# A layer kernel's first loads: the last three weight tiles of the shift as column sums, other buffers and order of the loads, and the token tiles' scale put into their transposing product

## The chip, the cores and the metric

One core of one Trainium2 chip runs the kernel. The metric is the device time of one execution in microseconds, the median of several executions.

## What is computed

One layer of a generator. 1024 latent tokens `x` and 256 context tokens `ctx`, each 1024 wide, are normalised, scaled and shifted (scale and shift come from `silu(c) @ w_ada`) and go through one input projection `w_in`; then come window attention, a chunked mLSTM, an output projection and a SwiGLU block. The change touches the beginning:

```python
mod_x = (silu_c @ w_ada[layer] + b_ada[layer])[:, None, :]      # 1024 -> 6 x 1024
mod_c = silu_cc @ w_ada[layer] + b_ada[layer]
sh_m, sc_m, gt_m, sh_f, sc_f, gt_f = jnp.split(mod_x, 6, axis=-1)
px = modulate(rms_norm(x, g_pre_mix[layer]), sh_m, sc_m) @ w_in[layer]     # h * (1 + sc) + sh
pc = modulate(rms_norm(ctx, g_pre_mix[layer]), csh_m, csc_m) @ w_in[layer]
```

Everything is float32. The large products are made from two float32r halves of each operand (`split`: the high half by a copy on ScalarE, the low one by a subtraction on VectorE) in three matmuls (`mm3`: high by high, high by low, low by high).

## The kernel before, in words

All DMAs are issued by one queue (SP), in the order that the program's scheduler gives them; `tc.issue_after(d)` keeps a load behind another one in that queue. The scheduler also orders the instructions of each engine. The stages at the start are these.

**Scale and shift (the loop `for sec in (1, 0)`).** Section 1 of `w_ada` gives the scale, section 0 the shift. Each section is eight tiles `wa` of 128x1024 (512 KB). An even tile is, in float32, the moving operand of two matmuls of 512 columns against `cz4`, four columns of silu values; an odd tile is split first and takes four float32r matmuls against `cs4`. All add into `pr`, two banks of four rows. At a section's end `pr` is copied to a tile of four rows `r4` (half by ScalarE, half by VectorE), turned into columns by eight small transposes (`pcol`), and a few VectorE instructions make `scol` (scale) or `hcol` (shift) of them.

**Token tiles (`prep_a`, `prep_b`).** There are ten tiles of 128 tokens, eight of `x` and two of `ctx`. `prep_a(i)` loads `xt`, squares and sums it on ScalarE, takes the root there and the reciprocal on VectorE, and multiplies the whole tile by it on GpSimd (line 187). `prep_b(i)` turns the tile over in eight TensorE transposes (`pt<-cst,xt`, line 200), multiplies by `scol` on VectorE (line 202), adds `hcol` on GpSimd (line 203; on VectorE for tile 0), and splits the result into `hh` and `hl` (`ch` and `cl` for the context), the stationary operands of the projection.

**First projection (`s1`, lines 70 to 72).** Per token tile 24 matmuls of 272 columns against `w1h` and `w1l`, whose weights come in four loads of 272 KB (`slab_load`) behind all of `w_ada`. The loop runs `prep_a(i + 4)`, `prep_b(i + 2)` and `s1(i)`. Token tiles and first projection together are called stage 1 below.

**Behind it** come the second projection (`w2h`, `w2l`, 384 columns), the gates' chain and the rest of the layer. In a name such as `pt<-cst,xt` of a matmul the moving operand stands first and the stationary one second.

Of the kernel before, what the change touches and what calls it, by code (L numbers as in the profile page):

```python
# [9 lines left out]
F32 = mybir.dt.float32  # L10
F32R = mybir.dt.float32r
# [26 lines left out]
def body(tc, x, ctx, vecs, bcv, bada, gqm, gqf, wada, ws1, ws2, wt, wout, wfi, wfo,  # L38
# [68 lines left out]
    act.activation(csil, vec[:, VSIL:VSIL + 16].rearrange("p (k t) -> p k t", t=2), AF.Silu)  # L107
    convw = vec[:, VCONV:VCONV + 12].rearrange("p (i t) -> p i t", t=3)
# [30 lines left out]
    pool.memset(Vc[:, :, :, 128:129], 1.0)  # L139
# [8 lines left out]
    ch = [R(i, f"ch{i}", (4, L), F32R) for i in range(2)]  # L148
    cl = [R(2 + i, f"cl{i}", (4, L), F32R) for i in range(2)]
# [11 lines left out]

# [10 lines left out]
    xts, hraw, xd = {}, {}, {}  # L172
# [6 lines left out]
    def prep_a(i):  # L179

        j = i - NT
        xt = xts[i] = R(4 + i % 4, f"xt{i}", (D,))
        xd[i] = dma(xt, x[i * P:(i + 1) * P] if i < NT else ctx[j * P:(j + 1) * P])
        hraw[i] = R((12, 13, 8, 9, 10, 11)[i % 6], f"hraw{i}", (KT, P))
        act.activation(hraw[i].rearrange("p a b -> p (a b)"), xt, AF.Square, accum_out=st[:, i:i + 1])
        rms_r(st[:, 10 + i:11 + i], st[:, i:i + 1])
        pool.tensor_scalar(xt, xt, st[:, 10 + i:11 + i], 1.0, MUL, MUL)

    def prep_b(i):

        xt = xts.pop(i)
        q, j = (0, i) if i < NT else (1, i - NT)
        hs, ls = (hh, hl) if i < NT else (ch, cl)
        tok = slice(j * P, (j + 1) * P)
        rw = hraw.pop(i)
        for b in range(2):
            pt = pa.tile([P, 4, P], F32, name="pt", tag="tp", bufs=2)
            for k in range(4):
                kk = 4 * b + k
                pe.transpose(pt[:, k, :], xt[:, kk * P:(kk + 1) * P], ident)  # L200
            raw = rw[:, 4 * b:4 * b + 4]
            dve.tensor_tensor(raw, pt, hcast(scol[:, q, 4 * b:4 * b + 4]), MUL)
            (dve if i == 0 else pool).tensor_tensor(raw, raw, hcast(hcol[:, q, 4 * b:4 * b + 4]), ADD)
            split(hs[b][:, :, tok], ls[b][:, :, tok], raw)
# [5 lines left out]

    for sec in (1, 0):
        pr = [pa.tile([4, 512], F32, name=f"pr{sec}{i}", tag="mm", bufs=4) for i in range(2)]
        for kt in range(KT):
            w = R((8, 9, 10, 11, 12, 13)[(kt + 2 * (1 - sec)) % 6], f"wa{sec}_{kt}", (D,))
            wd = dma(w, wada[kt * P:(kt + 1) * P, sec * D:(sec + 1) * D])
            if kt % 2:
                wh, wl = (w2_tile(p, kt // 2 % 2, f"wa{p}{sec}_{kt}")[:, 0:D] for p in "hl")
                split(wh, wl, w)
                ops = ((cs4, wh), (cs4, wl))
            else:  # L220
                ops = ((cz4, w),)
            for n, (a, b) in enumerate(ops):
                for i in range(2):
                    pe.matmul(pr[i], a[:, kt, :], b[:, i * 512:(i + 1) * 512], start=kt == 0,
                              stop=kt == KT - 1 and n == len(ops) - 1)
            if (sec, kt) == (1, 0):
                with tc.issue_after(wd.ins):
                    dma(cst, const)
                    dma(bcr, bcast(bcv))
                dve.tensor_scalar(mF, up, -1.0, -NEG, ADD, MUL)  # L230
                dve.tensor_scalar(mB, lw, -1.0, -NEG, ADD, MUL)
            if (sec, kt) == (0, 4):
                prep_a(0)
        r4 = R((7, 6)[sec], f"r4_{sec}", (D,))[0:4]
# [15 lines left out]
    with tc.issue_after(wd.ins):  # L250
        for i in range(2):
            slab_load(w1h[i], w1l[i], ws1[:, i], 272, 2 * i)
# [33 lines left out]
    with tc.issue_after(wd.ins):  # L286
        for n in range(1, 4):
            prep_a(n)
    for n in range(2):
        prep_b(n)  # L290
# [1486 lines left out]
```

## Time and profile before

| what | value |
| --- | --- |
| median of 3 executions (lowest to highest) | 1234.12 us (1230.72 to 1235.18) |
| the profiled execution: its time, its span | 1231.71 us, 1229.9 us |
| TensorE busy | 1193.5 us, 97% of the span |
| VectorE, ScalarE, GpSimd busy | 799.9, 578.1, 205.8 us |
| mean granted TensorE clock | 0.996 of full speed |

The profile is of one execution. PE is TensorE's matmuls, PEld its weight loads, DVE VectorE, ACT ScalarE, POOL GpSimd, SP the queue that issues the DMAs. A matmul's duration in a row holds its way through the array, so consecutive ones overlap: what one costs in a stream is the distance between starts. A float32 matmul of the program is two instructions in the rows (the 32 of line 224 on `wa,cz` are 16 of the program), a float32r matmul or a transpose is one.

### The profile page before, as it was taken

To read this page: it belongs to the slowest core of one execution; us is meant where nothing else is said; L and a number is where in the kernel's file an instruction comes from. 1 tells how busy PE (TensorE), PEld (TensorE's weight loads), DVE (VectorE), ACT (ScalarE), POOL (GpSimd) and SP (SyncE) were. 2 spreads that over 40 slices of the span, in tenths; PEclk is the share of its full clock that TensorE was granted. 3 is DMA by queue.
4 is the path that set the end of the run, shared out by engine and by line. 5 is a ranking of instruction groups with operands and counts; after the bars stand their busy time and mean duration, and the time that the engine had idled before them with its cause. 6 is when DMAs were issued, how large, how long until landed. Compare 5 with 4: busy or idle time off the path is not lost.

```text
span 1229.9 us, 16238 instructions
## 1 busy us (share of the span) xinstructions
PE 1193.5 (97%) x5859; PEld 968.9 (79%) x5859; DVE 799.9 (65%) x1385; ACT 578.1 (47%) x1105; POOL 205.8 (17%) x245
## 2 busy tenths in 40 slices
PE   7889999999999998999999999999999999999997
PEld 1779878877777776887778888888888888888886
DVE  3882177772877788446867677767777755554567
ACT  3754533211766786587643333334333334444443
POOL 0651410235544476000000000000000000000000
PEclk9899999999999999999999999999999999999999
DMA  8542854556533320522034465575645548665853
GB/s 313 168 132 70 280 188 144 181 145 191 153 90 87 112 78 10 188 86 86 18 104 136 180 218 198 204 246 195 230 141 177 176 162 279 205 205 188 299 188 129
DMA packets 91096, 202.30 MB, mean 164 GB/s; under 512 B 9092, under 2 KB 29956, under 8 KB 89608
## 3 DMA queue, kind: packets, MB, share of 16 engines
q1 hardware_dynamic: 91016, 201.27, 49.4%
q8 instruction: 46, 0.75, 0.2%
q14 instruction: 34, 0.28, 0.1%
HBM read 149.85 MB, written 50.73 MB: 163 GB/s over the span
## 4 chain that ended last, share of the span: by engine, by line
PE 78%; DMA 7%; DVE 7%; POOL 3%; ACT 3%; issue 2%; SPq 1%; DVEq 0%; POOLq 0%; ACTq 0%
PE xv L72 8%; PE xv L70 8%; PE xv L71 8%; PE pt L70 5%; PE pt L71 5%; PE pt L72 5%; PE pt L708 2%; PE pt L707 2%; PE pt L808 2%; DMA wb<-in_wada 2%; PE op L72 2%; PE fx L70 2%; PE fx L71 2%; PE fx L72 2%; PE op L71 2%
## 5 line engine op out<-in xcount | busy, mean ns | idle before, releaser
L59 DVE TENSOR_TENSOR fo<-fr,fo 128x1024 fp32r<-128x1024 f32 x77 | 92.7, 1222 | 70.9 <-ACT fo L58 67.7
L58 ACT CAST fo<-fr 128x1024 fp32r<-128x1024 f32 x77 | 79.5, 1050 | 74.0 <-PE pt L72 34.9
L441 PE MATMUL t<-hh,th 128*128 128x512 f32 x208 | 82.5, 397 | 1.8 <-ACT cr L458 1.8
L442 PE MATMUL t<-hl,th 128*128 128x512 f32 x208 | 82.1, 395 | 0.0
L1192 ACT CAST wS<-wr 128x512 fp32r<-128x512 f32 x88 | 54.1, 622 | 55.8 <-PE pt L72 37.5
L1194 DVE TENSOR_TENSOR wS<-wr,wS 128x512 fp32r<-128x512 f32 x88 | 60.3, 688 | 20.7 <-ACT wS L1192 20.7
L444 PE MATMUL t<-hh,tl 128*128 128x512 f32 x208 | 68.2, 393 | 0.0
L70 PE MATMUL xv<-tT,wS 128*128 128x512 f32 x168 | 66.0, 393 | 0.0
L72 PE MATMUL xv<-tT,wS 128*128 128x512 f32 x168 | 65.6, 391 | 0.0
L71 PE MATMUL xv<-tT,wS 128*128 128x512 f32 x168 | 65.5, 390 | 0.0
L492 DVE SCALAR_TENSOR_TENSOR acc<-wb,csil,acc 128x1024 f32<-128x1024 f32 x24 | 33.9, 1411 | 40.6 <-DMA wb<-in_wada 40.6
L441 PEld LDWEIGHTS t<-hh,th 128*128 128x128 f32 x208 | 39.1, 188 | 10.4 <-ACT cr L458 2.4
L944 DVE TENSOR_TENSOR wr<-wr 128x512 f32<-128x512 f32 x66 | 45.5, 689 | 1.4
L442 PEld LDWEIGHTS t<-hl,th 128*128 128x128 f32 x208 | 39.1, 188 | 8.1 <-issue 1.2
L1226 ACT ACTIVATE es<-es 128x512 f32<-128x512 f32 x22 | 13.9, 633 | 66.6 <-DVE es L947 66.6
L72 PE MATMUL op<-woh,ml 128*128 128x512 f32 x112 | 43.8, 391 | 0.8 <-DVE ml L59 0.8
L444 PEld LDWEIGHTS t<-hh,tl 128*128 128x128 f32 x208 | 38.3, 188 | 7.9 <-issue 1.0
L70 PE MATMUL op<-woh,mh 128*128 128x512 f32 x112 | 44.2, 395 | 0.0
L71 PE MATMUL op<-wol,mh 128*128 128x512 f32 x112 | 43.7, 390 | 0.0
L70 PE MATMUL pt<-fo 128*128 128x512 f32 x110 | 42.8, 389 | 0.0
L71 PE MATMUL pt<-fo 128*128 128x512 f32 x110 | 42.8, 389 | 0.0
L72 PE MATMUL pt<-fo 128*128 128x512 f32 x110 | 42.8, 389 | 0.0
(991 smaller groups left out, 3489.9 us busy)
## 6 DMA issues: line engine op xcount, KB each, us to landing
wr<-in_wfi SPq DMA_DIRECT2D x44, 512.0 KB, 4.8
wb<-in_wada SPq DMA_DIRECT2D x24, 512.0 KB, 4.3
s_d<-a SPq DMA_DIRECT2D x22, 512.0 KB, 6.6
bt<-in_wfo SPq DMA_DIRECT2D x44, 256.0 KB, 3.7
tb_d<-bt SPq DMA_DIRECT2D x11, 1024.0 KB, 4.1
fr<-s_d SPq DMA_DIRECT2D x44, 256.0 KB, 4.5
fr<-tb_d SPq DMA_DIRECT2D x44, 256.0 KB, 4.3
fr<-a_d SPq DMA_DIRECT2D x33, 256.0 KB, 4.2
```

The source lines that it names most:

```text
L58: act.copy(hi, raw)
L59: dve.tensor_tensor(lo, raw, hi.bitcast(F32), SUB)
L70: pe.matmul(ps, a[0], b[0], start=first, stop=False, **kw)
L71: pe.matmul(ps, a[0], b[1], start=False, stop=False, **kw)
L72: pe.matmul(ps, a[1], b[0], start=False, stop=last, **kw)
L441: pe.matmul(o, wh[:, kt], m[0], start=f, stop=False)
L442: pe.matmul(o, wh[:, kt], m[1], start=False, stop=False)
L444: pe.matmul(o, wl[:, kt], m[0], start=False, stop=l)
L492: dve.scalar_tensor_tensor(a, t, csil[:, kt, 0:1], a, MUL, ADD)
L944: dve.tensor_tensor(out, a, b, SUB)
L1192: act.copy(w[:, 0], raw)
L1194: dve.tensor_tensor(w[:, 1], raw, w[:, 0].bitcast(F32), SUB)
```

## The change

- Of section 0 (the shift) five tiles go through `pr`, tiles 1, 3 and 4 of them split. Tiles 5, 6 and 7 become stationary operands: for each of the eight 128-column blocks of a tile there is one float32 matmul against two columns of silu values (`pcc<-csil,wa`, line 293 after). The sums stand in columns at once, and VectorE adds them to `hcol` (line 296 after).
- `w_ada` has a buffer for each of a section's eight tiles instead of six. `xt0` is loaded behind tile 1 of section 0, `xt1` behind tile 4; then come the first half of `w1`'s weights, tiles 5 to 7, and the second half, each half as one load of 544 KB into a buffer of its own.
- `prep_a` no longer multiplies the token tile: GpSimd multiplies the 128x128 unit matrix by the reciprocal root (`dg`, line 189 after), and `prep_b` has, for each transpose, a float32 matmul of the tile with `dg` (`pt<-dg,xt`, line 203 after).
- A Sqrt activation is added at the start, some instructions are kept in program order, `r4` lies in the memory of `Vc`, and the low halves of the second half of `w1` are made between the splits of tile 0.

```diff
@@ -105,6 +105,7 @@
     up, lw = cst[:, CUP:CUP + P], cst[:, CLO:CLO + P]
     sel, ind = cst[:, CSEL:CSEL + P], cst[:, CIND:CIND + 64]
     act.activation(csil, vec[:, VSIL:VSIL + 16].rearrange("p (k t) -> p k t", t=2), AF.Silu)
+    act.activation(st[:, 63:64], epst, AF.Sqrt)
...
@@ -145,8 +145,7 @@
-    ch = [R(i, f"ch{i}", (4, L), F32R) for i in range(2)]
-    cl = [R(2 + i, f"cl{i}", (4, L), F32R) for i in range(2)]
+    ch, cl = [], []
...
@@ -158,7 +157,7 @@
+    q1.tile([P, P], F32, name="dgx", tag="dg", bufs=4)
...
@@ -181,57 +180,89 @@
         j = i - NT
         xt = xts[i] = R(4 + i % 4, f"xt{i}", (D,))
         xd[i] = dma(xt, x[i * P:(i + 1) * P] if i < NT else ctx[j * P:(j + 1) * P])
-        hraw[i] = R((12, 13, 8, 9, 10, 11)[i % 6], f"hraw{i}", (KT, P))
-        act.activation(hraw[i].rearrange("p a b -> p (a b)"), xt, AF.Square, accum_out=st[:, i:i + 1])
+        hraw[i] = R((2, 3)[i] if i < 2 else (12, 13, 8, 9, 10, 11)[i % 6], f"hraw{i}", (KT, P))
+        sq = act.activation(hraw[i].rearrange("p a b -> p (a b)"), xt, AF.Square, accum_out=st[:, i:i + 1])
+        if i > 1:
+            tc.keep_in_program_order(sq)
         rms_r(st[:, 10 + i:11 + i], st[:, i:i + 1])
-        pool.tensor_scalar(xt, xt, st[:, 10 + i:11 + i], 1.0, MUL, MUL)
-
-    def prep_b(i):
-
-        xt = xts.pop(i)
+        dg[i] = q1.tile([P, P], F32, name=f"dg{i}", tag="dg", bufs=4)
+        pool.tensor_scalar(dg[i], ident, st[:, 10 + i:11 + i], 1.0, MUL, MUL)
+
+    def prep_b(i, between=None):
+
+        xt, dg_ = xts.pop(i), dg.pop(i)
         q, j = (0, i) if i < NT else (1, i - NT)
         hs, ls = (hh, hl) if i < NT else (ch, cl)
         tok = slice(j * P, (j + 1) * P)
         rw = hraw.pop(i)
+        tail = []
         for b in range(2):
             pt = pa.tile([P, 4, P], F32, name="pt", tag="tp", bufs=2)
             for k in range(4):
                 kk = 4 * b + k
-                pe.transpose(pt[:, k, :], xt[:, kk * P:(kk + 1) * P], ident)
+                pe.matmul(pt[:, k, :], xt[:, kk * P:(kk + 1) * P], dg_, start=True, stop=True)
             raw = rw[:, 4 * b:4 * b + 4]
             dve.tensor_tensor(raw, pt, hcast(scol[:, q, 4 * b:4 * b + 4]), MUL)
             (dve if i == 0 else pool).tensor_tensor(raw, raw, hcast(hcol[:, q, 4 * b:4 * b + 4]), ADD)
-            split(hs[b][:, :, tok], ls[b][:, :, tok], raw)
+            tail.append((hs[b][:, :, tok], ls[b][:, :, tok], raw))
+            if i:
+                h_, l_, raw = tail.pop()
+                tc.keep_in_program_order(act.copy(h_, raw))
+                dve.tensor_tensor(l_, raw, h_.bitcast(F32), SUB)
+        for b, t in enumerate(tail):
+            split(*t)
+            between(2 * b)
...
 
+
+    w1r = {}
+
+    def w1_load(i):
+        w1r[i] = R(i, f"wr1_{i}", (4, 272))
+        return dma(w1r[i], ws1[:, i])
+
+    def w1_hi(i, k):
+        act.copy(w1h[i][:, k:k + 2], w1r[i][:, k:k + 2])
+
+    def w1_lo(i, k):
+        return dve.tensor_tensor(w1l[i][:, k:k + 2], w1r[i][:, k:k + 2], w1h[i][:, k:k + 2].bitcast(F32), SUB)
+
+    PLAIN = {1: (0, 2, 4, 6), 0: (0, 2)}
+    NROW = {1: KT, 0: KT - 3}
+    last, nsp = None, 0
     for sec in (1, 0):
         pr = [pa.tile([4, 512], F32, name=f"pr{sec}{i}", tag="mm", bufs=4) for i in range(2)]
-        for kt in range(KT):
-            w = R((8, 9, 10, 11, 12, 13)[(kt + 2 * (1 - sec)) % 6], f"wa{sec}_{kt}", (D,))
-            wd = dma(w, wada[kt * P:(kt + 1) * P, sec * D:(sec + 1) * D])
-            if kt % 2:
-                wh, wl = (w2_tile(p, kt // 2 % 2, f"wa{p}{sec}_{kt}")[:, 0:D] for p in "hl")
+        for kt in range(NROW[sec]):
+            w = R(8 + kt, f"wa{sec}_{kt}", (D,))
+            with tc.issue_after(last) if last is not None else ExitStack():
+                last = dma(w, wada[kt * P:(kt + 1) * P, sec * D:(sec + 1) * D]).ins
+            if kt in PLAIN[sec]:
+                ops = ((cz4, w),)
+            else:
+                wh, wl = (w2_tile(p, nsp % 2, f"wa{p}{sec}_{kt}")[:, 0:D] for p in "hl")
+                nsp += 1
                 split(wh, wl, w)
                 ops = ((cs4, wh), (cs4, wl))
-            else:
-                ops = ((cz4, w),)
             for n, (a, b) in enumerate(ops):
                 for i in range(2):
                     pe.matmul(pr[i], a[:, kt, :], b[:, i * 512:(i + 1) * 512], start=kt == 0,
-                              stop=kt == KT - 1 and n == len(ops) - 1)
+                              stop=kt == NROW[sec] - 1 and n == len(ops) - 1)
             if (sec, kt) == (1, 0):
-                with tc.issue_after(wd.ins):
+                with tc.issue_after(last):
                     dma(cst, const)
-                    dma(bcr, bcast(bcv))
+                    last = dma(bcr, bcast(bcv)).ins
                 dve.tensor_scalar(mF, up, -1.0, -NEG, ADD, MUL)
                 dve.tensor_scalar(mB, lw, -1.0, -NEG, ADD, MUL)
-            if (sec, kt) == (0, 4):
-                prep_a(0)
-        r4 = R((7, 6)[sec], f"r4_{sec}", (D,))[0:4]
+            if (sec, kt) in ((0, 1), (0, 4)):
+                i = kt // 4
+                with tc.issue_after(last):
+                    prep_a(i)
+                    last = xd[i].ins
+        r4 = Vc.rearrange("p n h v -> p (n h v)")[0:4, 0:D]
         act.copy(r4[:, 0:512], pr[0])
         dve.tensor_copy(r4[:, 512:D], pr[1])
         pc_ = pa.tile([P, KT, 4], F32, name="pcol", tag="gx", bufs=2)
@@ -247,9 +278,29 @@
                 dve.tensor_tensor(t, t, vec[:, VGPM:VGPM + 8], MUL)
             else:
                 dve.tensor_tensor(t, t, bcol(0), ADD)
-    with tc.issue_after(wd.ins):
-        for i in range(2):
-            slab_load(w1h[i], w1l[i], ws1[:, i], 272, 2 * i)
+        if sec == 0:
+            with tc.issue_after(last):
+                last = w1_load(0).ins
+            for k in (0, 2):
+                w1_hi(0, k)
+                w1_lo(0, k)
+            pcc = pa.tile([P, KT, 2], F32, name="pcc", tag="mm", bufs=4)
+            for kt in range(NROW[0], KT):
+                w = R(8 + kt, f"wa{sec}_{kt}", (D,))
+                with tc.issue_after(last):
+                    last = dma(w, wada[kt * P:(kt + 1) * P, 0:D]).ins
+                for j in range(KT):
+                    pe.matmul(pcc[:, j, :], w[:, j * P:(j + 1) * P], csil[:, kt, :], start=kt == NROW[0] and j == 0,
+                              stop=kt == KT - 1, skip_group_check=j > 0)
+    for q in range(2):
+        dve.tensor_tensor(hcol[:, q], pcc[:, :, q], hcol[:, q], ADD)
+    pool.memset(Vc[:, :, :, 128:129], 1.0)
+    with tc.issue_after(last):
+        last = w1_load(1).ins
+    for k in (0, 2):
+        w1_hi(1, k)
+    ch += [R(i, f"ch{i}", (4, L), F32R) for i in range(2)]
+    cl += [R(2 + i, f"cl{i}", (4, L), F32R) for i in range(2)]
@@ -283,11 +334,13 @@
 
     NI = NT + NC_
     w2h, w2l = [], []
-    with tc.issue_after(wd.ins):
-        for n in range(1, 4):
+    prep_b(0, lambda k: tc.keep_in_program_order(w1_lo(1, k)))
+    for n in (2, 3):
+        with tc.issue_after(last):
             prep_a(n)
-    for n in range(2):
-        prep_b(n)
+        last = xd[n].ins
+        if n == 2:
+            prep_b(1)
     for i in range(NI):
         if i + 4 < NI:
             prep_a(i + 4)
```

Where the instructions stand. On TensorE, from the transposes of tile 0 to the first projection, before (`xt_248`, `xt_313` and `xt_320` are the token tiles 0, 1 and 2):

```order
L200 MATMUL pt<-cst,xt_248 128x128 x6
L224 MATMUL pr_214<-wal_7_272,cs_126 4x512
L224 MATMUL pr_215<-wal_7_272,cs_126 4x512
L239 MATMUL pcol<-cst,r_0_279 128x4 x8
L200 MATMUL pt<-cst,xt_313 128x128 x8
L70 MATMUL slab<-w1h_121,hh_101 128x272
L71 MATMUL slab<-w1l_123,hh_101 128x272
L200 MATMUL pt<-cst,xt_320 128x128 x8
L72 MATMUL slab<-w1h_121,hl_103 128x272
```

and in the changed kernel (`xt_258` is token tile 1; `pr_210` and `pr_211` are section 0):

```order
L252 MATMUL pr_210<-wah_4_250,cs_123 4x512
L252 MATMUL pr_211<-wah_4_250,cs_123 4x512
L252 MATMUL pr_210<-wal_4_251,cs_123 4x512
L252 MATMUL pr_211<-wal_4_251,cs_123 4x512
L270 MATMUL pcol<-cst,Vc 128x4 x4
L203 MATMUL pt<-dg_264,xt_258 128x128 x8
L270 MATMUL pcol<-cst,Vc 128x4 x4
L293 MATMUL pcc<-csil,wa_5_290 128x2 x8
L293 MATMUL pcc<-csil,wa_6_300 128x2 x8
L293 MATMUL pcc<-csil,wa_7_310 128x2 x8
L70 MATMUL slab<-w1h_117,hh_101 128x272
```

The products of tile 1 and the column sums of three tiles now stand ahead of the first projection, in this order, and the turning of token tile 2 no longer stands right behind its first two matmuls.

On VectorE, at the end of the shift, in the changed kernel (`hraw_228` is token tile 0, `w1l_120` the second half of `w1`):

```order
L280 TENSOR_TENSOR hcol<-hcol,vec 128x8 x2
L296 TENSOR_TENSOR hcol<-pcc,hcol 128x8 x2
L206 TENSOR_TENSOR hraw_228<-hraw_228,hcol 128x512 x2
L59 TENSOR_TENSOR hl_103<-hraw_228,hh_101 128x4x128
L232 TENSOR_TENSOR w1l_120<-wr_1_323,w1h_118 128x2x272
L59 TENSOR_TENSOR hl_104<-hraw_228,hh_102 128x4x128
L232 TENSOR_TENSOR w1l_120<-wr_1_323,w1h_118 128x2x272
```

The addition of the column sums is the last step ahead of token tile 0, whose splits and the rest of `w1l` stand behind it.


## Rows read from the trace of the kernel before

**Rows 1.** Busy time of each engine in three stretches of the span (start:end, length, then busy us and count of PE, PEld, DVE, ACT and POOL, the granted clock as a share of full speed, the DMA engines' share and GB/s).

```profile
40.00:50.00 10.00, 8.63 (x54) 8.01 (x54) 9.93 (x16) 8.25 (x18) 9.21 (x7) 0.74 0.44 152
42.20:84.20 42.00, 36.91 (x273) 35.01 (x274) 37.71 (x72) 25.71 (x56) 35.28 (x29) 0.96 0.42 129
84.20:163.00 78.80, 78.35 (x444) 71.88 (x443) 24.98 (x59) 37.27 (x96) 22.84 (x22) 1.00 0.54 180
```

**Rows 2.** Groups of instructions in the stretch from 42.2 to 84.2 us (line, engine, operation, tiles, shapes, count | busy us, mean ns | idle before them and what ended it).

```profile
L203 POOL TENSOR_TENSOR hraw<-hraw,hcol 128x512 f32<-128x512 f32 x18 | 25.2, 1410 | 6.6 <-DVE hraw L202 6.6
L72 PE MATMUL slab<-w1h,hl 128*128 128x272 f32 x64 | 19.5, 307 | 3.3 <-DVE hl L59 3.3
L187 POOL TENSOR_SCALAR xt<-xt,st 128x1024 f32<-128x1024 f32 x8 | 11.9, 1484 | 1.8 <-PE pt L200 1.8
L202 DVE TENSOR_TENSOR hraw<-pt,scol 128x512 f32<-128x512 f32 x17 | 11.4, 675 | 0.0
L200 PE MATMUL pt<-cst,xt 128*128 128x128 f32 x64 | 10.3, 293 | 0.2 <-POOL xt L187 0.2
L70 PE MATMUL slab<-w1h,ch 128*128 128x272 f32 x6 | 1.8, 307 | 1.5 <-ACT ch L58 1.5
```

**Rows 3.** PE in order of time, at the shift's matmuls and at the start of the first projection (start us, busy us, engine, line, operation, tiles, shapes, count, idle before).

```profile
24.25 0.75 PE L239 MATMUL pcol<-cst,r 4*128 4x4 f32 x8
...
26.28 1.88 PE L224 MATMUL pr<-wa,cz 128*4 128x512 f32 x4
28.09 0.63 PE L224 MATMUL pr<-wah,cs 128*4 128x512 f32 x2
...
29.11 1.88 PE L224 MATMUL pr<-wa,cz 128*4 128x512 f32 x4
...
42.23 0.60 PE L70 MATMUL slab<-w1h,hh 128*128 128x272 f32 x1 [1.19 <-ACT hh L58]
...
42.85 1.91 PE L200 MATMUL pt<-cst,xt 128*128 128x128 f32 x8
44.41 0.58 PE L72 MATMUL slab<-w1h,hl 128*128 128x272 f32 x1
...
45.21 0.28 PE L72 MATMUL slab<-w1h,hl 128*128 128x272 f32 x1
45.34 0.29 PE L70 MATMUL slab<-w1h,hh 128*128 128x272 f32 x1
45.46 0.29 PE L71 MATMUL slab<-w1l,hh 128*128 128x272 f32 x1
```

**Rows 4.** PE in order of time, a group of eight transposes in the middle of stage 1, and what follows it.

```profile
49.69 1.09 PE L200 MATMUL pt<-cst,xt 128*128 128x128 f32 x8 [0.18 <-POOL xt L187]
50.54 0.37 PE L72 MATMUL slab<-w1h,hl 128*128 128x272 f32 x1
```

**Rows 5.** PE in order of time in the mLSTM stage: float32 matmuls of 129 columns, each of the program's as two instructions.

```profile
343.31 0.49 PE L708 MATMUL pt<-V,wl 128*128 128x129 f32 x2
343.73 0.49 PE L707 MATMUL pt<-cs,qp 64*128 64x129 f32 x2
344.14 0.49 PE L708 MATMUL pt<-V,wl 128*128 128x129 f32 x2
```

**Rows 6.** PE in order of time: eight float32 matmuls of one column with 128x128 stationary operands, and what follows them.

```profile
193.45 1.84 PE L508 MATMUL ar<-one,acc 128*128 128x1 f32 x16
195.16 0.48 PE L442 MATMUL t<-hl,th 128*128 128x512 f32 x1
```

**Rows 7.** ACT in order of time: two copies that waited for their `w_ada` tile (tile 1 of section 1, tile 1 of section 0), the copy of a section's sums, a square with its read-out, the root with the table load ahead of it, the copy that waited for the last `w_ada` tile, and two copies of a half token tile.

```profile
9.01 1.04 ACT L58 CAST wah<-wa 128x1024 fp32r<-128x1024 f32 x1 [6.08 <-DMA wa<-in_wada]
...
20.68 1.05 ACT L58 CAST wah<-wa 128x1024 fp32r<-128x1024 f32 x1 [1.62 <-DMA wa<-in_wada]
23.62 0.58 ACT L235 COPY r<-pr 4x512 f32<-4x512 f32 x1 [1.89 <-PE pr L224]
...
28.20 1.06 ACT L185 ACTIVATE hraw<-xt 128x1024 f32<-128x1024 f32 x1 [2.92 <-PE pr L224]
29.16 0.19 ACT L185 ACTIVATION_READ_ACCUMULATOR hraw<-xt 128x1 f32 x1
...
30.30 1.28 ACT L176 ACT_TABLE_LOAD   x1
31.59 0.29 ACT L176 ACTIVATE st<-st,epst 128x1 f32<-128x1 f32 x1
32.38 1.04 ACT L58 CAST wah<-wa 128x1024 fp32r<-128x1024 f32 x1 [0.49 <-DMA wa<-in_wada]
...
41.58 1.12 ACT L58 CAST hh<-hraw 128x512 fp32r<-128x512 f32 x2
```

**Rows 8.** DVE in order of time: a reciprocal, the shift's last step, and the addition of the shift to half a token tile.

```profile
31.92 0.17 DVE L177 RECIPROCAL st<-st 128x1 f32<-128x1 f32 x1 [0.38 <-ACT st L176]
39.07 0.25 DVE L249 TENSOR_TENSOR hcol<-hcol,vec 128x8 f32<-128x8 f32 x2
39.88 0.68 DVE L203 TENSOR_TENSOR hraw<-hraw,hcol 128x512 f32<-128x512 f32 x1
```

**Rows 9.** POOL in order of time: the nearest smaller and larger size of a product by a column.

```profile
7.53 0.20 POOL L637 TENSOR_SCALAR bcr<-bcr 128x8 f32<-128x8 f32 x1 [6.12 <-DMA bcr<-in_bcv]
37.90 1.12 POOL L187 TENSOR_SCALAR xt<-xt,st 128x1024 f32<-128x1024 f32 x1 [4.61 <-DVE st L177]
```

More of the change, by code (lines that the diff above doesn't have):

```diff
@@ L138, in body @@
     pool.memset(V[:, :, :, 128:129], 1.0)
-    pool.memset(Vc[:, :, :, 128:129], 1.0)
     pool.memset(G, 0.0)
@@ L170, in w2_tile @@
         return q1.tile([P, 4 * 384], F32R, name=name, tag=f"w2{part}{i}")
-    xts, hraw, xd = {}, {}, {}
+    xts, hraw, xd, dg = {}, {}, {}, {}
     def rms_r(dst, ss):
```

## The prediction, made before the change was run

> **What bounds the kernel now.** I read the busy time by stretches first: it tells in which part of the span TensorE has room [rows 1]. From 84.2 to 163 us PE is busy 78.35 of 78.80 us, and the whole page has it at 97%. So a microsecond that the start wins or loses is passed on to the end nearly whole. From 42.2 to 84.2 us three engines are close together: PE 36.91, DVE 37.71 and POOL 35.28 of 42.00 us. The groups of that stretch say what PE lacks there [rows 2]: its matmuls waited 3.3 us for `hl`, 1.5 us for the context's `ch` and 0.2 us for `xt`, 5.0 us together. Behind those waits stands GpSimd, with 1484 ns for each scaled tile and two additions of 1410 ns, 4.3 us a token tile. Third, PE in order of time gives the start of the first projection [rows 3]: its first matmul is at 42.23. Two things are to be seen behind it. The transposes of token tile 2 (the third one) take from 42.85 to 44.41, 1.56 us, and the five slab matmuls around them are slow: 42.23 to 42.85 (two) and 44.41 to 45.21 (three) are 1.42 us, where the later ones start 0.125 us apart (45.21 to 45.46), 0.62 for five. That is 0.8 us lost; the stretch from 40 to 50 has a granted clock of 0.74 [rows 1], a mixture of the levels 1.2 and 2.4 GHz.
>
> **The price of turning a tile.** Before, eight transposes take 0.85 us in the stream (49.69 to 50.54), 0.106 each [rows 4]. After, each is an ordinary float32 matmul with a 128x128 stationary operand and 128 moving columns. The nearest row is the mLSTM's: 128x128 against 129 columns, two instructions, from one pair to the next 0.42, 0.41 us [rows 5]. I take 0.417 us: 3.34 us a tile instead of 0.85. Lower bound: the columns alone, without any weight load. 512 float32 columns are 0.45 us an instruction (26.28 to 28.09 for four) [rows 3], 128 columns twice are 0.226 us. Upper bound: the pair's own 0.49 us [rows 5]. I take the middle because shape, type and stream are the same there.
>
> A rule bears on this. In the row, the columns explain 0.226 of 0.417 us, and the rest is what a weight load costs when it stands alone: eight matmuls of one column take 1.71 us (193.45 to 195.16), 0.107 us an instruction [rows 6]. So in float32 the loads of successive blocks were not hidden. The Trainium skill, TensorE: Matmul & The Clock Gate, Part 2: What happens when you issue a matmul, says that the engine pulls a weight load ahead of matmuls that are under way, so that the next weights load meanwhile. By that rule a product would cost its columns alone, and the sum below would end near 1235 us instead of 1248. The pairs' 0.417 us speak against it here.
>
> **The change, part by part.**
>
> Until PE has done the first copies of tile 1 of the shift, the order on PE is the same, so I keep 24.25 us for the start of `pcol` [rows 3] and walk from there in the new order. Half of `pcol` 0.4 (half of 0.75), the low half of tile 1 0.5 (half of 28.09 to 29.11), tile 2 of the shift 1.8, the other half of `pcol` 0.4: 27.35. `dg` of token tile 0 must be there: the copy of the sums ends at 24.2, square and read-out 1.25, table load 1.28, root 0.29 [rows 7], reciprocal 0.17 [rows 8], and the product of the unit matrix between 0.20 (8 columns) and 1.12 us (1024 columns) [rows 9]; with 128 columns I take 0.3. That is 27.5, and the Sqrt at the program's start does not remove the table load, since the Silu behind it loads another table. Products of tile 0 3.34: 30.85. Shift tiles 3 and 4, both split, 2.0: 32.85. Copy of the sums 0.6: 33.45, half of `pcol` 33.85. Products of tile 1 3.34: 37.2, `pcol` 37.6. Then the column sums: 24 float32 matmuls, 48 instructions of 0.107 us [rows 6], 5.1: 42.7. The row has one column, here are two; were they as dear as 129 columns it would be 10.0, were they free 0. Then 0.25 for the two additions to `hcol`, 0.68 for the shift of half a tile [rows 8], 0.6 for its copy (41.58, two in 1.12) [rows 7] and 0.25 for hand-overs: the first projection starts at 44.5 instead of 42.23, **+2.3**.
>
> The loads do not set this. Between 9.01 and 20.68 nine loads of 512 KB landed, 1.30 us each [rows 7]. In the new order tile 7 of the shift comes 16 such loads and one of 544 KB (1.4) behind tile 1 of section 1: 31.2, against 32.38 before [rows 7], though `xt1` and half of `w1` now stand ahead of it in SP's queue. PE comes to it after 40 us; a slip of 8 us in the queue costs nothing. The second half of `w1` lands at 32.6 and token tile 2 at 33.9, also early. Two SP issues fewer for `w1`, and two splits of 128x1024 fewer with one more for tile 4, are worth nothing for the same reason: ScalarE and VectorE have waits in that stretch. If PE were not late, those loads would be the bound.
>
> Token tiles 2 to 9: 64 transposes of 0.106 become 64 products of 0.417: **+19.9**. The transposes of tile 2 that stood behind the first two slab matmuls were slow, 1.56 instead of 0.85, so another **-0.7** goes; the slow slab matmuls go too, if the clock stays up: **-0.8**. (The ramp of PE from 24.25 to 42.7 has no wait over 0.6 us.)
>
> GpSimd loses 1.48 us a tile and gets 0.3: 3.1 us. PE now has 24 slab matmuls, 3.0, and 3.34, 6.3 us a tile, above GpSimd's 3.1 and VectorE's 4.5 (37.71 us for the stretch, some eight tiles). So PE alone paces stage 1 and the 5.0 us of waits go: **-5.0**. New is a wait at the start: the second half of `w1l` stands between the low halves of tile 0 on VectorE. Four steps of about 0.8 (the addition to half a tile is 0.68 [rows 8]) end at 47.7, where PE has by then done 26 slab matmuls, 3.25 us from 44.5: **+1.0**, between 0 and 5.0 (all of the old waits' sum).
>
> Behind stage 1 nothing is changed but the order of some `w_dr` transfers, and the gates' chain starts as late as stage 1 ends, so PE and that chain move together.
>
> Sum: 2.3 + 19.9 - 0.7 - 0.8 - 5.0 + 1.0 = **+16.7**. Against the profiled execution, 1231.7, this is 1248.4; the median shown is 2.4 us above that execution, so the same sum against the median would be 1250.8. I take **1249 us**, slower by 1.2%. (0.5%, 6.2 us, is about what a measurement of this kernel can tell from no change.)
>
> **The rivals.**
>
> A, not slower: the weight loads of the products are hidden, so that a product costs 0.226. There are 80 products on PE's path (16 in the ramp, 64 behind it): 80 x 0.19 = 15.3 us less. PE is then near GpSimd's and VectorE's pace, and I leave 2.5 us of the waits instead of 1.0: 1248.4 - 15.3 + 1.5 = 1235. For it: a float32r slab matmul does start every 0.125 us with its own weight load [rows 3]. Against it: [rows 5] and [rows 6]. It decides from 0.30 us a product downwards (16.7 - 80 x 0.12 = 7.1 us left), at 0.21 nothing is left. Chance 0.09; in a quarter of that the products are as cheap as transposes and the waits stay away: 16.7 - 80 x 0.311 = -8.2, 1223.
>
> B, slower still: the clock falls. Before, it did so where PE had several waits of about 1 us in a row between 36 and 42 us, one of them the 1.19 us in [rows 3], and it came back at 45.2. If the waits at 27.4, 32.9 and 42.7 to 44.5 do the same, the second group of products, the column sums and the first 26 slab matmuls (3.3 + 5.1 + 3.3) run at 1.2 GHz, at most 11.7 us more; with half of it 1254 to 1255. Against it: PE is busier here than it was there. Chance 0.14.
>
> **How the numbers follow.** Forecast 0.77, B 0.14, A 0.09. The range takes in the product's upper bound (80 x 0.073 = 5.8), B's 6 and waits of 5.0 instead of 1.0, not all at once: 1257. Downwards cheaper column sums (half, 2.5), no new wait (1.0) and a ramp that is shorter by 3 to 4 us, which its walk may miss: 1241. A stands outside. Slower takes the forecast, B and none of A (0.91, less 0.03 for a sum that ends under 1240): 0.88; same 0.09; faster 0.03.
>
> **What would show it.** In the profile after: pairs of `pt<-dg,xt` instructions 0.42 us apart; the first slab matmul at 44 to 45 us, with the column sums right ahead of it and their tiles landed long before; hardly any wait of PE between 50 and 100 us; GpSimd's idle time for VectorE up; stage 1 ending some 16 us later and all stages behind it as long as before. Products 0.3 us apart or less, or a first slab matmul before 40 us, would prove me wrong.

## The result

The changed kernel takes 1238.34 us (median of 12 executions, 1236.27 to 1239.98) where the kernel before, beside it on the same chip, took 1231.62: a ratio of 1.005, 95% interval 1.0037 to 1.0062. It is slower by 4.6 to 7.6 us, not by the 16.7 of the sum. The profiled execution took 1237.45 us with a span of 1235.7, 5.8 more than before; all that follows is set against this 5.8.

### The profile page after: what moved, and what is told of

Its sections match the earlier page's. It is cut to its first block, busy times and chain, and to the rows that moved or that the text cites. A ratio compares the mean times of both kernels' runs of the same rounds, so it can differ in the third digit from the quotient of the medians.

```text
span 1235.7 us, 16466 instructions
## 1 busy us (share of the span) xinstructions
PE 1202.5 (97%) x5975; PEld 984.7 (80%) x5975; DVE 794.9 (64%) x1386; ACT 578.4 (47%) x1106; POOL 194.7 (16%) x245
## 4 chain that ended last, share of the span: by engine, by line
PE 87%; DMA 4%; DVE 4%; ACT 3%; issue 1%; POOL 1%; SPq 0%; DVEq 0%; POOLq 0%; ACTq 0%
PE xv L72 8%; PE xv L70 8%; PE xv L71 8%; PE pt L72 5%; PE pt L71 5%; PE pt L70 5%; PE t L495 3%; PE t L494 3%; PE t L497 3%; PE pt L761 2%; PE pt L760 2%; PE pt L861 2%; PE op L72 2%; PE fx L70 2%; PE fx L72 2%; PE fx L71 2%
```

## The profile after

In the changed kernel the products of the scaled tiles are L203, the column sums L293, their addition to `hcol` L296, `dg` L189, the addition of the shift L206. PE in order of time, from the shift to the second group of products in stage 1 (start, busy, line, tiles, shapes, count, idle before), answers to [rows 3, 4]:

```profile
22.69 0.41 PE L270 MATMUL pcol<-cst,Vc 4*128 4x4 f32 x4
...
26.01 2.05 PE L203 MATMUL pt<-dg,xt 128*128 128x128 f32 x16 [0.20 <-POOL dg L189]
27.82 0.70 PE L252 MATMUL pr<-wah,cs 128*4 128x512 f32 x2
...
30.78 2.05 PE L203 MATMUL pt<-dg,xt 128*128 128x128 f32 x16
32.77 0.41 PE L270 MATMUL pcol<-cst,Vc 4*128 4x4 f32 x4
33.10 7.52 PE L293 MATMUL pcc<-csil,wa 128*128 128x2 f32 x48
42.25 0.59 PE L70 MATMUL slab<-w1h,hh 128*128 128x272 f32 x1 [1.63 <-ACT hh L58]
42.65 0.43 PE L71 MATMUL slab<-w1l,hh 128*128 128x272 f32 x1
44.49 0.59 PE L72 MATMUL slab<-w1h,hl 128*128 128x272 f32 x1 [1.42 <-DVE hl L59]
44.89 0.43 PE L70 MATMUL slab<-w1h,hh 128*128 128x272 f32 x1
45.11 0.43 PE L71 MATMUL slab<-w1l,hh 128*128 128x272 f32 x1
...
49.87 0.33 PE L72 MATMUL slab<-w1h,hl 128*128 128x272 f32 x1
50.04 1.95 PE L203 MATMUL pt<-dg,xt 128*128 128x128 f32 x16
51.74 0.37 PE L72 MATMUL slab<-w1h,hl 128*128 128x272 f32 x1
```

Three things are to be seen. Eight products take 1.81 us (26.01 to 27.82) in the ramp and 1.70 us (50.04 to 51.74) in stage 1, 0.226 and **0.213 us each**, not 0.417. The 48 instructions of the column sums take 7.5 us instead of 5.1. And the slab matmuls begin at 42.25, where they began before, but stand 0.227 apart up to 49.87; before, they were 0.125 apart from 45.21 on.

The stretches, those of [rows 1] and the one ahead of them (columns as there):

```profile
30.00:40.00 10.00, 9.62 (x70) 9.40 (x71) 4.04 (x12) 2.58 (x5) 0.48 (x2) 0.82 0.64 253
40.00:50.00 10.00, 6.95 (x29) 6.54 (x30) 7.16 (x13) 6.29 (x13) 4.97 (x5) 0.50 0.00 0
42.20:84.20 42.00, 40.53 (x313) 40.21 (x314) 32.70 (x68) 27.20 (x59) 24.91 (x24) 0.91 0.36 114
84.20:163.00 78.80, 77.32 (x446) 71.18 (x445) 20.89 (x59) 37.05 (x97) 23.97 (x25) 1.00 0.51 169
```

The granted clock from 40 to 50 us is 0.50, the lower level all along, where it was 0.74. From 42.2 to 84.2 PE is now busy 40.53 of 42.00 us instead of 36.91, and GpSimd 24.91 instead of 35.28.

What PE waited for after 20 us (engine, tile, line <- releaser: us, times, longest), which answers to the idle column of [rows 2]:

```profile
PE t L494 <- ACT cr L508: 1.7, 1, 1.7
PE t L494 <- ACT cr L511: 1.7, 2, 1.1
PE slab L70 <- ACT hh L58: 1.6, 1, 1.6
PE slab L72 <- DVE hl L59: 1.4, 1, 1.4
...
PE slab L70 <- ACT ch L210: 0.4, 1, 0.4
```

Of the old 3.3 us for `hl` one wait at the start is left, and 0.4 of the 1.5 for `ch`. The waits for `cr` come long after stage 1; before they were 1.8 us in all, here 3.4.

## The experiments

Each ran beside the kernel before on the same chip, and a ratio is to that kernel. The chips differ from one group of runs to the next, so two runs are set against each other by their ratios (0.1% is 1.2 us).

**1. What does a product cost, and why was the row that I took dearer?**

In the changed kernel, plain transposes of the unscaled tile in place of the products (the tokens stay unscaled):

```
-                pe.matmul(pt[:, k, :], xt[:, kk * P:(kk + 1) * P], dg_, start=True, stop=True)
+                pe.transpose(pt[:, k, :], xt[:, kk * P:(kk + 1) * P], ident)
```

> The changed kernel with plain transposes of the unscaled token tiles in place of the products with the scaled identity (GpSimd still makes it, nobody reads it; the tokens go on unscaled, so the values are not the reference's). It measures the products' own price. If each product costs 0.107 more than a transpose and TensorE is the bound from 50 to 163 us: 64 x 0.107 = 6.8 less than the changed kernel, 1231.5, unless the lower clock of the ramp or other waits take some of it: 1231 to 1234. If the prediction's 0.31 a product held: 20 less, 1218. If the products are hidden: 1238.

Measured: 1230.17 us, ratio 0.9986 (0.9974 to 0.9999), by the ratios 7.9 us under the changed kernel. That fits what the products' instructions take, 64 x 0.107 = 6.8 in stage 1 and 8.6 with the 16 of the ramp, and nothing hides them. (The two profiled spans are 7.0 us apart, but these executions do not start alike: the high half of tile 1 of the shift is multiplied at 22.09 in the changed kernel and at 23.90 here; what lies behind that is told where the prediction's ramp is answered.) The run also gives what the rest of the change is worth when GpSimd's scaling is gone as well and nothing stands in its place: 0.1 to 3.2 us.

Then the price of [rows 5]. In the kernel before, L707 (64 rows) and L708 (128 rows) alternate. First grouped in pairs:

```
-            pe.matmul(pv[:, j, :], qp_[r, d, j, :], cs[r, j, :], start=True, stop=False)
-            pe.matmul(pv[:, j, :], wt_[:, d, 2 * j + hb, :], V[:, n, 2 * j + hb, :], start=False, stop=True)
+            pe.matmul(pv[:, j, :], qp_[r, d, j, :], cs[r, j, :], start=True, stop=False, skip_group_check=True)
+        for j in range(2):
+            pe.matmul(pv[:, j, :], wt_[:, d, 2 * j + hb, :], V[:, n, 2 * j + hb, :], start=False, stop=True, skip_group_check=True)
```

> The kernel before, in which the four value products of a token tile, direction and head half stand as L707, L707, L708, L708 instead of L707, L708, L707, L708 (the same 256 products of 129 columns in all, the same sums). It asks where the 0.42 us of a product came from that the prediction took over from [rows 5]. Theory 1: the price is paid at each passage between a stationary operand of 64 rows (L707) and one of 128 rows (L708); with half as many passages, each worth 0.42 less 0.21, the 128 groups of products seen in the trace cost 64 x 0.21 = 13 us less, on a TensorE that is busy 98% of this stretch: near 1219 against 1232. Theory 2: it is the price of any float32 product with a load of its own, or of the accumulation in pairs: no change, 1232 within 2, and the products still 0.42 us each.

(The 256 are instructions; the products are 128. The sums do not stay the same: in this order the values are not the reference's, so the run tells of the time only.) PE in order of time in that run:

```profile
338.82 0.71 PE L707 MATMUL pt<-cs,qp 64*128 64x129 f32 x4
339.46 0.71 PE L709 MATMUL pt<-V,wl 128*128 128x129 f32 x4
340.10 0.71 PE L707 MATMUL pt<-cs,qp 64*128 64x129 f32 x4
```

Two products in 0.64 us instead of 0.84: half of the surcharge is gone, as theory 1 had it. The time did not follow: 1229.57 us, ratio 0.9980 (0.9965 to 0.9994). The last L707 starts at 426.0 instead of 437.8, but from 470 to 480 us PE then waits for VectorE (1.9 us and 2.9 us) at a granted clock of 0.66, and the span is only 4.9 us shorter. Second, L707 over all 128 rows (its values then hold both heads' sums):

```
-            pe.matmul(pv[:, j, :], qp_[r, d, j, :], cs[r, j, :], start=True, stop=False)
+            pe.matmul(pv[:, j, :], qp_[:, d, j, :], cs[:, j, :], start=True, stop=False)
```

> The kernel before, in which L707 contracts over all 128 rows of qp and of the state instead of the 64 rows of one head (so its values hold both heads' sums; nothing else differs, the products' number, order and columns stay). Theory 1 (the passage between 64 and 128 rows costs): the products stand 0.21 us apart, the trace's 256 of them cost 128 x 0.42 - 128 x 0.21 = 27 us less per 128 seen, of which other engines may take some back: between 1204 and 1215. Theory 2 (accumulation in pairs, or 129 columns, or the load of its own): no change, 1232 within 2.

PE in order of time in that run:

```profile
344.09 0.38 PE L707 MATMUL pt<-cs,qp 128*128 128x129 f32 x2
344.31 0.39 PE L708 MATMUL pt<-V,wl 128*128 128x129 f32 x2
344.53 0.39 PE L707 MATMUL pt<-cs,qp 128*128 128x129 f32 x2
344.75 0.39 PE L708 MATMUL pt<-V,wl 128*128 128x129 f32 x2
```

0.22 us each instead of 0.42, with the same number, order, columns and accumulation: 1210.64 us, ratio 0.9831 (0.9812 to 0.9849), 21 us of the 128 x 0.2 = 25 that PE is spared. So the price that I took over was that of the passage between stationary operands of 64 and of 128 rows, 0.2 us each. The Trainium skill, TensorEngine Tiling (Array Packing), Key Properties, says that a change of the tiling mode drains the engine; it gives no time for it. The two runs fit it if operands of 64 and of 128 rows count as two such modes; no trace here shows the drain itself. The products of this change have 128 rows throughout and pay none of that.

**2. The column sums, the clock and the new order.**

In the changed kernel, the two moving columns repeated 32 times:

```
-            pcc = pa.tile([P, KT, 2], F32, name="pcc", tag="mm", bufs=4)
+            pcc = pa.tile([P, KT, 64], F32, name="pcc", tag="mm", bufs=4)
...
-        pe.matmul(pcc[:, j, :], w[:, j * P:(j + 1) * P], csil[:, kt, :], ...
+        csw = csil[:, kt, :].rearrange("p (o t) -> p o t", o=1).broadcast_to([P, 32, 2])
+        pe.matmul(pcc[:, j, :], w[:, j * P:(j + 1) * P], csw, ...
```

> The changed kernel, with 64 instead of 2 moving columns in the column sums (the same two silu columns repeated 32 times; same 24 matmuls, same loads of the stationary operand). Theory 1 (the clock fell from 2.4 to 1.2 GHz because 48 instructions of two columns leave TensorE nearly without work): the 48 instructions take 5.1 us instead of 7.5, the first slab matmul is at 39.9 instead of 42.25, and the slab matmuls behind it start 0.125 us apart instead of 0.227 until 49.9; 2.4 + 2.5 = 4.9 us less, about 1233.5. Theory 2 (the clock fell because of the waits of 1.6 and 1.4 us between 40.5 and 44.5): the sums still take 7.5 us, the slabs are still slow, the time stays within 1 us of 1238.3.

PE in order of time in that run:

```profile
33.06 5.57 PE L294 MATMUL pcc<-csil,wa 128*128 128x64 f32 x48
40.27 0.59 PE L70 MATMUL slab<-w1h,hh 128*128 128x272 f32 x1 [1.63 <-ACT hh L58]
...
42.51 0.60 PE L72 MATMUL slab<-w1h,hl 128*128 128x272 f32 x1 [1.42 <-DVE hl L59]
...
46.07 0.43 PE L72 MATMUL slab<-w1h,hl 128*128 128x272 f32 x1
```

and its stretches (columns as in [rows 1]):

```profile
30.00:40.00 10.00, 8.30 (x72) 7.94 (x72) 5.33 (x16) 2.94 (x6) 1.56 (x3) 1.00 0.64 251
40.00:50.00 10.00, 8.31 (x47) 7.99 (x48) 7.20 (x15) 7.27 (x16) 4.30 (x6) 0.66 0.00 1
```

With 64 columns the same 48 instructions take 5.57 us instead of 7.52, and the granted clock from 30 to 40 us is 1.00 instead of 0.82: with two columns each the sums ran part of their time at the lower level. The first slab matmul comes 2.0 us earlier. But behind it the slab matmuls are slow again, 0.227 apart up to 46 us: PE, nearly idle from 38.6 to 42.5, finds the lower level there too (0.66 from 40 to 50 us). 1236.73 us, ratio 1.0036 (1.0022 to 1.0049): by the ratios 1.7 us less than the changed kernel, which the two intervals do not separate from nothing; in the profiles the one-column matmuls of [rows 6] come 1.55 us earlier (197.77 for 199.32).

All eight tiles of the shift by row sums again, with the rest as changed:

```
-    PLAIN = {1: (0, 2, 4, 6), 0: (0, 2)}
-    NROW = {1: KT, 0: KT - 3}
+    PLAIN = {1: (0, 2, 4, 6), 0: (0, 2, 4, 6)}
+    NROW = {1: KT, 0: KT}
...
```

> The changed kernel, with all eight tiles of the shift through the row sums again (tiles 1, 3, 5, 7 split), loads in the changed order, products kept. Theory 1 (the column sums bring the clock down): no 7.5 us of column sums, 3.8 us of row sums and about 2.5 us of copy, small transposes and additions behind them instead, granted clock 1.00 from 30 to 36; first slab matmul at 38 to 39; slabs mostly at full clock: 1232 to 1233. Theory 2 (waits bring it down): first slab matmul at 38 to 39, but the waits of 3 to 4 us ahead of it lower the clock and 2.5 us of slow slabs stay: 1235.

Measured: 1237.46 us, ratio 1.0045 (1.0030 to 1.0059), the first slab matmul at 41.03 us. That is more than either theory had, with the first slab matmul later than both had it. It cannot be told from the changed kernel: within some 2 us the column sums give nothing here and cost nothing.

In the changed kernel, GpSimd's scaling of the whole tile and the transposes again:

```
-        pool.tensor_scalar(dg[i], ident, st[:, 10 + i:11 + i], 1.0, MUL, MUL)
+        pool.tensor_scalar(xt, xt, st[:, 10 + i:11 + i], 1.0, MUL, MUL)
-                pe.matmul(pt[:, k, :], xt[:, kk * P:(kk + 1) * P], dg_, start=True, stop=True)
+                pe.transpose(pt[:, k, :], xt[:, kk * P:(kk + 1) * P], ident)
```

> The changed kernel, with the token tiles scaled on GpSimd and turned over by transposes again; column sums, buffers and order of the loads as changed. Theory 1 (a product costs 0.213 us against 0.106 of a transpose, and the 5.0 us of waits in stage 1 come back): 64 x 0.107 = 6.8 us less in stage 1 and 1.7 less in the ramp, 5 us of waits more: 3 to 4 us less, about 1235. Rival (what GpSimd is spared is worth more than the products cost): 1239 to 1242. The clock is as low as in the changed kernel from 36 to 50 us under either, since the column sums are left in.

Measured: 1238.97 us, ratio 1.0050 (1.0034 to 1.0067), the same as with the products, so the rival was nearer. PE again waits for `hl` (3.2 us) and `hh` (0.7) in stage 1 and for `xt` (1.0) in the ramp, 4.9 us, and the first slab matmul comes at 44.31 instead of 42.25. From the run with transposes of the unscaled tile (0.9986) this one differs only in GpSimd's scaling of the tile (there it makes the small `dg`, which nobody reads): that scaling costs 7.9 us by the ratios, and the products that replace it cost the same 7.9.

In the kernel before, the products alone:

```
+        dg[i] = q1.tile([P, P], F32, name=f"dg{i}", tag="dg", bufs=4)
-        pool.tensor_scalar(xt, xt, st[:, 10 + i:11 + i], 1.0, MUL, MUL)
+        pool.tensor_scalar(dg[i], ident, st[:, 10 + i:11 + i], 1.0, MUL, MUL)
-                pe.transpose(pt[:, k, :], xt[:, kk * P:(kk + 1) * P], ident)
+                pe.matmul(pt[:, k, :], xt[:, kk * P:(kk + 1) * P], dg_, start=True, stop=True)
```

> The kernel before, with only the products in place of the scaled tile and the transposes. If a product costs 0.213 us: 64 x 0.107 = 6.8 us more, up to 5.0 us of waits for GpSimd less: 1.5 to 3 us slower than before, 1233 to 1235. If it cost 0.417 us as in the mLSTM rows, 14 us slower, 1246.

Measured: 1239.53 us, ratio 1.0056 (1.0039 to 1.0074): dearer than I expected, since the first slab matmul comes at 46.60 instead of 42.23. VectorE in order of time shows a part of why:

```profile
41.47 0.18 DVE L243 COPY col<-pcol 128x32 f32<-128x32 f32 x1
42.70 0.16 DVE L178 RECIPROCAL st<-st 128x1 f32<-128x1 f32 x1 [1.05 <-ACT st L177]
42.78 0.24 DVE L246 TENSOR_TENSOR hcol<-col 128x8 f32<-128x8 f32 x2
...
44.26 0.68 DVE L205 TENSOR_TENSOR hraw<-hraw,hcol 128x512 f32<-128x512 f32 x1
```

The scheduler now puts three token tiles ahead of the shift's end; a later tile's reciprocal waits 1.05 us for its root, and `hcol`, on which all tiles hang, is queued behind it. The shift's `pcol` too stands behind the products of tile 1, at 39.72 instead of 37.80 for its last half. In the changed kernel the first slab matmul is back at 42.25, but its time (1.0050) cannot be told from this run's: its other order is worth less than the start says.

**3. Can the empty TensorE at 40 to 44 us be filled?**

In the changed kernel ScalarE is idle for 8 us there and then squares token tile 2 (ACT in order of time):

```profile
41.58 0.62 ACT L58 CAST hh<-hraw 128x512 fp32r<-128x512 f32 x1 [8.35 <-DVE hraw L206]
43.03 0.62 ACT L58 CAST hh<-hraw 128x512 fp32r<-128x512 f32 x1 [0.83 <-DVE hraw L206]
43.55 1.05 ACT L184 ACTIVATE hraw<-xt 128x1024 f32<-128x1024 f32 x1
```

So the loads and squares of tiles 2 and 3 went ahead of tile 0's conversion, alone and with the wide sums:

```
-    prep_b(0, lambda k: tc.keep_in_program_order(w1_lo(1, k)))
     for n in (2, 3):
         with tc.issue_after(last):
             prep_a(n)
         last = xd[n].ins
-        if n == 2:
-            prep_b(1)
+    prep_b(0, lambda k: tc.keep_in_program_order(w1_lo(1, k)))
+    prep_b(1)
```

> The changed kernel, in which the loads and squares of token tiles 2 and 3 stand ahead of the first token tile's conversion in the program, so that ScalarE squares them in the 8.35 us in which it was idle before hh at 41.58, and the products of token tile 2 can run while TensorE waits for the first hl (42.65 to 44.49). Theory 1 (the ramp loses by the empty TensorE after the column sums): the 1.7 us of those products leave the later stage, and the low clock of the first 24 slab matmuls ends sooner: 1.5 to 3 us less than the changed kernel, 1235 to 1237. Theory 2 (the clock is lost already in the column sums, and the products cost the same wherever they stand): within 1 us of the changed kernel, 1238.

> The changed kernel with the early squares and with the column sums as products of 64 columns (the two columns repeated 32 times), both together. If the two causes of the low clock add: the 1.6 us that the wide sums alone brought, and 1.5 to 3 more: 1233 to 1235, so no slower than the kernel before by more than 3. If one covers the other: 1236 to 1237. The products' 64 x 0.107 = 6.8 us and the 5.0 us of waits that they save stay in both.

Measured: 1240.03 (ratio 1.0067, 1.0049 to 1.0086) and 1237.93 us (1.0052, 1.0036 to 1.0068). Neither came out as hoped. GpSimd in the second of them:

```profile
38.71 2.98 POOL L206 TENSOR_TENSOR hraw<-hraw,hcol 128x512 f32<-128x512 f32 x2 [5.57 <-DVE hcol L297]
41.67 2.69 POOL L189 TENSOR_SCALAR dg<-cst,st 128x128 f32<-128x128 f32 x2
```

`dg` of tile 2 stands behind two additions that wait for the column sums, so its products come at 43.08 us instead of right behind the sums, at 38.4. In the next run `prep_a(2)` and `prep_a(3)` stand ahead of the addition of the column sums, and so their reciprocal on VectorE and `dg` on GpSimd too:

```
+    for n in (2, 3):
+        with tc.issue_after(last):
+            prep_a(n)
+        last = xd[n].ins
     for q in range(2):
         dve.tensor_tensor(hcol[:, q], pcc[:, :, q], hcol[:, q], ADD)
...
```

> The kernel of the early squares with wide sums, in which the reciprocal and the scaled identity of token tiles 2 and 3 stand ahead of the addition of the column sums on VectorE and GpSimd (before, they were queued behind it and the products of tile 2 came only at 43.08). Now these products stand between the column sums and the first slab matmul, where TensorE was empty. If the empty TensorE at 38.4 to 43 is what the ramp loses: the 1.7 us of products leave the later stage and the slow slab matmuls are gone: 2 to 4 us less than the wide sums alone (1236.7), 1233 to 1235. If the first hl and the waits behind it set the start of the stage whatever TensorE does: 1236 to 1238.

PE in order of time in that run:

```profile
34.85 5.57 PE L294 MATMUL pcc<-csil,wa 128*128 128x64 f32 x48
40.26 2.00 PE L203 MATMUL pt<-dg,xt 128*128 128x128 f32 x16
42.06 0.40 PE L70 MATMUL slab<-w1h,hh 128*128 128x272 f32 x1
42.30 0.29 PE L71 MATMUL slab<-w1l,hh 128*128 128x272 f32 x1
44.11 2.05 PE L203 MATMUL pt<-dg,xt 128*128 128x128 f32 x16 [1.52 <-POOL dg L189]
45.91 0.37 PE L70 MATMUL slab<-w1h,hh 128*128 128x272 f32 x1
```

and one of its stretches:

```profile
40.00:50.00 10.00, 8.48 (x70) 8.26 (x70) 9.54 (x15) 4.75 (x9) 6.27 (x5) 1.00 0.30 106
```

The products of tile 2 fill the gap (a wait of 1.5 us for the next `dg` is left), the granted clock from 40 to 50 us is 1.00, and no slab matmul is slow: 1234.81 us, ratio 1.0030 (1.0019 to 1.0042). By the ratios that is 2.5 us less than the changed kernel, just clear of the noise, and 0.7 less than the wide sums alone, which is not.

**4. A version that beats both.** In the kernel before, q of each head in a tile whose other 64 rows are zero, so that L707 has 128 rows with the right values; then the same in the kernel of the last run:

```
-        qps[n] = R((13, 15)[n % 2], f"qp{n}", (2, 2, P))
+        if n < 2:
+            qps[n] = R((13, 15)[n % 2], f"qp{n}", (2, 2, 2, P))
+            for hb in range(2):
+                pool.memset(qps[n][64 - hb * 64:P - hb * 64, hb], 0.0)
+        else:
+            qps[n] = qps[n - 2]
...
-            pe.matmul(pv[:, j, :], qp_[r, d, j, :], cs[r, j, :], start=True, stop=False)
+            pe.matmul(pv[:, j, :], qp_[:, hb, d, j, :], cs[:, j, :], start=True, stop=False)
```

> The kernel before, in which q of each head is loaded into a tile whose other 64 rows are zero, so that L707 contracts over 128 rows with the reference's values. New are 4 memsets, and 4 loads of 64 rows for each token tile instead of 2 of 128. If the price of [rows 5] is the passage between 64 and 128 rows: as the run with all rows, 1210 to 1213. If the extra loads or memsets are waited for: up to 1220. If the earlier gain came from the values and not from the rows: 1232.

> The changed kernel with the zero rows, the wide sums and the scaled identities of tiles 2 and 3 ahead. The stages lie apart, so the gains should add: 21 less than the same kernel without zero rows, 1212 to 1215; above the kernel before with zero rows by what the products still cost, 1 to 4. If the clock or a wait behind takes back: up to 1220.

Measured: 1215.94 us, ratio 0.9880 (0.9863 to 0.9898), and 1222.13, 0.9925 (0.9912 to 0.9939). The first beats both kernels, by 15 and (by the ratios) some 21 us. So the gain comes from the rows and not from the values; it is some 6 us less than with all rows. GpSimd there, and then PE, each in order of time:

```profile
309.97 1.09 POOL L681 MEMSET qp<- 64x512 f32 x2 [11.84 <-DMA so_d<-so]
```

```profile
314.11 0.90 PE L815 MATMUL pt<-cst,pr__2717 128*128 128x128 f32 x3 [3.59 <-POOL pr__2717 L801]
```

The second tile's memset waits until a store has left its buffer, and the attention's first steps on GpSimd queue behind it; PE waits 3.6 us and then runs from 315 to 320 us at a granted clock of 0.57. In the second kernel that wait is 4.4 us, and the clock is 0.77 from 320 to 330. The second kernel is above the 1220 that I had allowed, and the 6 us between the two are more than the 3.7 by which it stands above the kernel before without the zero rows. In the profiles they lie ahead of the attention: the one-column matmuls of [rows 6] are at 190.86 and 196.98, and 1.6 us of these 6.1 stand already at `pcol` (22.47 and 24.05), a difference of single executions, as told below.

## Why the prediction was wrong, and where it was right

The direction was right and the size was not. By its own terms, predicted and measured:

- **The products, +19.9: +6.8.** This is the step that failed. "I take the middle because shape, type and stream are the same there" holds for shape and type, not for the stream: half of the 0.417 of [rows 5] was the passage between 64 and 128 rows, which these products don't make (runs 1). Its lower bound, 0.226, was nearly right, and the neighbour that agrees was [rows 6]: 0.107 an instruction with a single column, 0.106 with 128. So an instruction's columns and its weight load do not add up here, and [rows 6] spoke for rival A, not against it. The rule that I set aside (the Trainium skill, TensorE: Matmul & The Clock Gate, Part 2: What happens when you issue a matmul) agrees with the trace after: 0.213 us a product, near the 0.226 of the columns alone.
- **The ramp, +2.3: +1.6, and another -1.6 that is not the change's.** From `pcol` to the first slab matmul I had 20.25 us; it is 19.56, against 17.98 before. The two groups of products cost 2.9 less, the column sums at the lower clock 2.4 more (7.5 instead of 5.1). That the first slab matmul stands at 42.25, where it stood before, is luck: `pcol` starts at 22.69, not 24.25. The four float32 instructions of tile 2 of section 1 show where that comes from. In order, one line each before and after, and two in the run with L707 over all rows, whose program is the one before up to there:

```profile
12.31 2.92 PE L224 MATMUL pr<-wa,cz 128*4 128x512 f32 x4
```

```profile
11.79 1.88 PE L252 MATMUL pr<-wa,cz 128*4 128x512 f32 x4
```

```profile
11.75 1.88 PE L224 MATMUL pr<-wa,cz 128*4 128x512 f32 x4
...
22.65 0.74 PE L239 MATMUL pcol<-cst,r 4*128 4x4 f32 x8
```

In the profiled execution of the kernel before, PE does them at the slower pace, and behind them it waits for no load up to `pcol`. The same program in the run with all rows does them at full pace and has `pcol` at 22.65; in the run of the grouped pairs they are slow, with a granted clock of 0.50 from 12 to 14 us, and `pcol` is at 24.25 again. (The clock record of the profile before has 1.00 there; the pace speaks against it.) So this 1.6 us changes from one execution to another, and the order of the loads shows no part in it.

- **Slow transposes, -0.7: gone as said. Slow slab matmuls, -0.8: +2.1 instead.** From 42.25 to 50.04 are 26 of them; without the hole of 1.6 us they took 6.2 us where 26 x 0.125 is 3.25, 2.9 lost against 0.8 before. That is rival B's mechanism: with the sums' 2.4 it cost 5.3 of the 11.7 us that B had at most. Of B's three places the first two, 27.4 and 32.9, hardly had a wait (0.20 and 0.43); it came from the narrow column sums and the empty 40.6 to 44.5 us: the wide sums keep the clock up until they end (runs 2), and with the gap filled as well no slab matmul is slow (runs 3).
- **Waits of stage 1, -5.0: -4.6**, as GpSimd's busy time and the waits show. **New wait at the start, +1.0: +1.6** (42.87 to 44.49). It came for the first `hl`, not for `w1l`.
- **Behind stage 1, 0: +1.6.** The copies `cr` on ScalarE stand in another order and PE waits 3.4 us for them instead of 1.8. I had said that only the `w_dr` transfers move there.

The sum of what was measured is 6.8 + 1.6 - 1.6 - 0.7 + 2.1 - 4.6 + 1.6 + 1.6 = 6.8, against the span's 5.8; 1.0 us is not assigned. Without the luck of the start the two profiles would be some 7.4 us apart; the medians are 6.7. With the start level, the span's difference arises between the first slab matmul and 199.32 us (the eight one-column matmuls of [rows 6], before at 193.45, 5.9 earlier), and stays.

So the direction was right, and in part for the reasons forecast: the products, the ramp and the new wait less the waits spared make 5.4 us (6.8 + 1.6 + 1.6 - 4.6). The clock (2.1 - 0.7) and the `cr` waits (1.6), forecast at nothing or less, make 3.0 more, and the luck of the start takes 1.6 back. Rival A's price was the right one, with B's clock on top. Over A's own 1235 the clock put 2.9 and 2.4 us and the later waits 1.6; the earlier start took 1.6 back, and other terms, not told apart here, the rest.

## What to carry to other kernels

Before taking a price from a neighbouring row, ask what stands between that row and its neighbours: here the surcharge belonged to the change between 64- and 128-row operands, and a stream of one kind alone (the one-column sums, the transposes) gave the right price. A step that moves work from a second engine to the bound one is worth only what it spares that one: by the ratios 7.9 us of products bought 7.9 us of GpSimd's scaling, of which 4.9 us are seen as waits of TensorE. A gap at the start costs twice, once as itself and once in the lower clock behind it, and work to fill it must be ahead in every queue that it passes, not only on its first engine. And before an earlier start is credited to a change, look at it in a kernel that the change leaves alone there.

## What the runs showed of the hardware

- In streams at full clock, float32 matmuls with 128x128 stationary operands cost nearly the same with few columns as with 129: 0.107 us an instruction with one [rows 6], 0.116 at most with 64 (5.57 us for 48), 0.106 to 0.113 with 128, 0.111 with 129; two instructions make a product. A transpose is one, 0.106.
- A passage between stationary operands of 64 and 128 rows cost 0.2 us in float32, 25 us of this kernel's TensorE time.
- With 48 such instructions of 2 columns in a row, 7.5 us, the granted clock fell to the lower level (0.82 from 30 to 40 us, 0.50 from 40 to 50); with 64 columns it was 1.00 until they ended.
- The first float32 matmuls ran at either pace in executions of the same program up to there: four instructions took 1.81 us with all rows and 2.85 in the kernel before, and `pcol` came at 22.65 or 24.25.
